# Taking turns between the two halves of an FFN chunk, product by product, in a streaming encoder layer

## The chip, the cores and the metric

The kernel runs on one core of a Trainium2 chip. The metric is device time in microseconds (us) for one launch: 2391.49 us before the change (median of three runs, 2389.07 to 2395.47).

## The reference

One Conformer-style layer for 1024 prompt frames and 32 sample frames, computed together as 1056 columns in fp32. The change touches only the two half-step FFNs, with D_MODEL 1024 and D_FF 2816:

```python
def _swiglu_half_step(x, g_pre, g_post, w_in, w_out):
    h = _rmsnorm(x, g_pre)
    gate, up = jnp.split(h @ w_in, 2, axis=-1)
    return x + 0.5 * _rmsnorm((jax.nn.silu(gate) * up) @ w_out, g_post)
...
x = _swiglu_half_step(x, g_ffn1_pre[l], g_ffn1_post[l], w_ffn1_in[l], w_ffn1_out[l])
# ... combined projection, conv branch, recurrent branch, merge ...
x = _swiglu_half_step(x, g_ffn2_pre[l], g_ffn2_post[l], w_ffn2_in[l], w_ffn2_out[l])
```

## The kernel before

All data is channels first: 128 channels on the partitions, columns (frames) along the free dimension. The 1056 columns are four quarters of 264. Every fp32 operand is split into a high and a low part (`split`: a copy by ScalarE, L91, then a subtraction by VectorE, L88), and every product is three matmuls, high by high, high by low, low by high (`mm3`, L202 to L204).

D_FF is cut into 22 chunks of 128 gate and 128 up channels. The first three chunks of FFN 1 (two of FFN 2) are ordinary products. The rest use a seven-product scheme on 2 x 2 blocks: the weight of a chunk (gate and up rows, two halves of the input channels) and the input (two halves of the input channels, an even and an odd quarter). `w_ops` makes seven weights w1 to w7 from the loaded rows w_g and w_u, by sums s and s3 on VectorE and a split each; w1, w2, w4 are blocks as loaded, w5, w6, w7, w3 need sums. `swiglu` does the seven products for one pair of quarters, called a half of the chunk here: 7 x 12 = 84 matmuls. Four PSUM tiles take part. p1 is product 1, then product 2 is added; p5 is product 5, copied to SBUF as s5; p6 starts as ScalarE's copy of p1 and gets product 6, then p7 starts as a copy of p6; VectorE adds s5 to p6; product 7 goes to p7, product 3 to p6, product 4 to p7. SiLU of p1 and p6 times the up values p7 and p7 + s5 (read after product 7) gives the hidden values `prod`, stored to DRAM (`hd`). `ffn` runs both halves of a chunk one after the other with the same weights, so a chunk is 168 matmuls. Then the output products read `hd` back (`hf`, split into hh and hl) with weights w_o.

What sets the order: the program's instructions are ordered by a scheduler that takes them by priority, which is the order of writing unless `tc.high_priority(offset=n)` moves an instruction up by n places, and by its own idea of when they are ready. On each engine they then run in exactly that order. Weight loads and weight splits have such offsets (`WAHEAD`, `WLATE`, `OAHEAD`); the copies and sums in PSUM have none. Pools limit what can be open: 6 PSUM banks for products, 3 raw weight buffers (a chunk takes two), 12 weight buffers (a chunk takes seven), 6 double tiles for weight sums and `prod`, 4 temporary tiles. All loads and stores are issued by SP's queue.

Of the kernel before, what the change touches and what calls it, by code (L numbers as in the profile page):

```python
# [10 lines left out]
AF = mybir.ActivationFunctionType  # L11
OP = mybir.AluOpType
# [8 lines left out]
N = T // NQ  # L21
# [11 lines left out]
UNIT = 1088  # L33
NU, NRING, NRAW, NTMP, NMID = 29, 12, 3, 4, 6

AHEAD, WAHEAD, WLATE, HAHEAD, OAHEAD = 350, 120, 100, 100, 150


SQ, TURN, CHAIN, MUW, LNW, STAG = 12, 6, 30, 16, 32, 32
# [13 lines left out]
def macaron_kernel(ctx: ExitStack, tc: tile.TileContext, a: dict, o: dict):  # L53
    nc = tc.nc
# [20 lines left out]
    def PAIR(dt, name):  # L75
        return up.tile([P, 2, 2 * N], dt, tag="u", name=name, padded_shape=[P, 2, UNIT // 2])

    def MID(name):
        return mp.tile([P, 2, N], F32, tag="m", name=name)

    def TMP(name):
        return tp.tile([P, N], F32, tag="t", name=name)

    def BANK(name):
        return ps.tile([P, 512], F32, tag="ps", name=name)

    def tt(out, x, y, op):
        return nc.vector.tensor_tensor(out, x, y, op=op)  # L88

    def copy(out, x):  # L90
        return nc.scalar.activation(out, x, AF.Copy)  # L91
# [27 lines left out]
    st = cp.tile([P, KC, H1 + H2 + 1], F32, name="st")  # L119
# [60 lines left out]
    def block(src, name, ahead=AHEAD, lead=0):  # L180
        with tc.high_priority(offset=ahead):
            with tc.high_priority(offset=lead):
                w = raw_block(src, name)
            h, l = (ring.tile([P, D], F32R, tag="r", name=f"w{x}_{name}") for x in "hl")
            split(h, l, w)
        return h, l
# [7 lines left out]
    def drain():  # L194
        while later:
            later.pop(0)[1]()
# [4 lines left out]
    def mm3(out, wh, wl, xh, xl, first, last):  # L201
        nc.tensor.matmul(out, wh, xh, start=first, stop=False, skip_group_check=True)  # L202
        nc.tensor.matmul(out, wh, xl, start=False, stop=False, skip_group_check=True)  # L203
        newest_mm[:] = [nc.tensor.matmul(out, wl, xh, start=False, stop=last, skip_group_check=True).ins]  # L204
        terms[0] += 1
        for e in [e for e in later if e[0] <= terms[0]]:
            later.remove(e)
            e[1]()
# [132 lines left out]
    def behind_parts(instructions):  # L341
        s = ExitStack()
        for ins in instructions:
            s.enter_context(tc.issue_after(ins))
        return s
# [50 lines left out]
            op("3", s)  # L396
        return r

    def swiglu(w, x, prod, name):

        def bank(k):
            return BANK(f"p{k}_{name}")[:, :N]

        def product(k, b, first):
            for j in range(HC):
                s = slice(j * P, (j + 1) * P)
                mm3(b, w[k][:, 0, s], w[k][:, 1, s], x[k][0][:, j, :], x[k][1][:, j, :], first and j == 0, j == HC - 1)  # L410

        s5, g0, g1, u1 = (TMP(f"{n}_{name}") for n in ("s5", "g0", "g1", "u1"))
        p1, p5 = bank("1"), bank("5")
        product("1", p1, True)
        p6 = bank("6")
        copy(p6, p1)
        product("5", p5, True)
        copy(s5, p5)
        product("6", p6, False)
        p7 = bank("7")  # L420
        copy(p7, p6)
        tt(p6, p6, s5, OP.add)
        product("2", p1, False)
        nc.scalar.activation(g0, p1, AF.Silu)
        product("7", p7, False)
        tt(u1, p7, s5, OP.add)
        product("3", p6, False)
        nc.scalar.activation(g1, p6, AF.Silu)  # L428
        product("4", p7, False)
        tt(prod[:, 1, :], g1, u1, OP.mult)  # L430
        return tt(prod[:, 0, :], g0, p7, OP.mult).ins


    def ffn(x, f, h, first, mid, w_in, w_out, early, between, finish, tail, n):
        hd = dp.tile([NF, P, T], F32, name=f"hd{n}")

        def hidden(i, w, c):
            prod = MID(f"prod{n}_{i}_{c}")
            last = swiglu(w, x[c], prod, f"{n}_{i}_{c}")
            nc.sync.dma_start(hd[i, :, 2 * N * c:2 * N * (c + 1)], prod)  # L440
            return last

        first(0, h)
        if n == 1:
            drain()
        q0 = list(newest_part) if n == 1 else []
        blks = []
        np = NP[n - 1]
        for i in range(np):
            with behind_parts(q0 if i else []):  # L450
                blks.append([block(w_in[2 * i + j], f"i{n}_{i}_{j}", AHEAD if n == 2 else 0, 2000 if n == 1 else 0) for j in range(2)])
        for q in range(NQ):
            if q + 1 < NQ:
                first(q + 1, h)
            if q not in h:
                drain()
            for i in range(np):
                pg = gemm(blks[i][0], h, q, f"pg{n}_{i}_{q}")
                pu = gemm(blks[i][1], h, q, f"pu{n}_{i}_{q}")
                t = TMP(f"si{n}_{i}_{q}")  # L460
                nc.scalar.activation(t, pg, AF.Silu)
                tt(t, t, pu, OP.mult)
                nc.sync.dma_start(hd[i, :, q * N:(q + 1) * N], t)
            if q >= 2:
                x_sums(x[q - 2], f[2 * q - 4], f[2 * q - 3], f"{n}_{q - 2}")
        for i in range(np, NF):
            with behind_parts(q0 if i == np else []):
                w = w_ops(w_in[2 * i], w_in[2 * i + 1], f"{n}_{i}", WAHEAD if i < np + 2 else WLATE)
            hidden(i, w, 0)
            end = hidden(i, w, 1)  # L470
            if i == 4:
                with tc.issue_after(end):
                    mid()

        sq = {}
        for c in range(2):
            hid = []
            for g in range(NF // 2):
                with tc.high_priority(offset=HAHEAD):
                    w = PAIR(F32, f"hf{n}_{c}_{g}")  # L480
                    nc.sync.dma_start(w, hd[2 * g:2 * g + 2, :, 2 * N * c:2 * N * (c + 1)].rearrange("k p n -> p k n"))
                    hi, lo = PAIR(F32R, f"hh{n}_{c}_{g}"), PAIR(F32R, f"hl{n}_{c}_{g}")
                    split(hi, lo, w)
                hid.append((hi, lo))
            y = {q: [QUAD(F32, f"y{n}_{q}_{h}") for h in range(2)] for q in (2 * c, 2 * c + 1)}
            for t in (t for q in y for t in y[q]):
                nc.gpsimd.memset(t[:, 0, 0:1], 0.0)
            if c == 1:
                for q in y0:
                    after(q * STAG, lambda q=q, y0=y0: early(q, y0[q], sq[q]))  # L490
            y0 = y

            def out(tiles, blks, which, c=c, hid=hid, y=y):

                b = {t: BANK(f"po{n}_{t[0]}_{t[1]}")[:, :N] for t in tiles}
                for k in range(NF):
                    hi, lo = hid[k // 2]
                    for m, q in tiles:
                        i = m * NF + k
                        if i // KC not in blks:  # L500
                            blks[i // KC] = block(w_out[i // KC], f"o{n}_{which}_{i // KC}", OAHEAD)
                        s = slice((q % 2) * N, (q % 2 + 1) * N)
                        mm(b[m, q], blks[i // KC], i % KC, hi[:, k % 2, s], lo[:, k % 2, s], k == 0, k == NF - 1)
                for m, q in tiles:
                    evacuate(y[q], m, b[m, q], half[:, n - 1, m:m + 1], sq, q, f"{n}_{q}_{m}")

            qs = (2 * c, 2 * c + 1)
            late = tail if c == 1 else 0
            both = {}
            out([(m, q) for m in range(OG) for q in qs], both, c)  # L510
            for m in range(OG, KC - late):
                for q in qs:
                    out([(m, q)], both, c)
                if c == 1 and m == HC - 1:
                    between()
            for q in qs:
                own = {}
                for m in range(KC - late, KC):
                    out([(m, q)], own, f"{c}_{q}")
                if c == 1 and q == 2:  # L520
                    finish(q, y[q], sq[q])
        return lambda: finish(3, y[3], sq[3])
# [146 lines left out]
    for i in range(KC):  # L669
        first, last = i == 0, i == KC - 1  # L670
# [21 lines left out]
        for k in range(H2):  # L692
            s = H2 - k
# [20 lines left out]
        for c0, cn in RCH:  # L714
            for j, dst in ((0, tau), (1, v)):
                b = BANK(f"pgt{i}_{c0}_{j}")[:, :cn]
# [29 lines left out]
        for q in range(NQ):  # L746
            p = gemm(br, hm, q, f"prg{i}_{q}")
            g = TMP(f"gl{i}_{q}")
            nc.scalar.activation(g, p, AF.Gelu_apprx_tanh)
            for lo, hi, to in pieces(q, H2):  # L750
                s = slice(to, to + hi - lo)
# [77 lines left out]
    for h in range(2):  # L829
        some = [co_row(h * HC + j) for j in range(HC)]  # L830
        for q in range(NQ):
            mg = QUAD(F32, f"mg{q}_{h}")
            s = slice(q * N, (q + 1) * N)
            for j, (b, g, r) in enumerate(some):
                p = gemm(b, hc, q, f"pco{h}_{j}_{q}")
# [107 lines left out]
```

## Time and profile before

| | before |
|---|---|
| runs (median, lowest, highest) | 2391.49, 2389.07, 2395.47 us |
| profiled execution | 2396.18 us, its span 2394.4 us |
| TensorE busy, granted clock | 2350.4 us (98%), mean 0.996 |
| VectorE, ScalarE busy | 1468.3 us (61%), 980.3 us (41%) |
| seven-product stage, FFN 1 and FFN 2 | 91.8 to 495.2 us, 1685.4 to 2108.7 us |

In the rows PE is TensorE, DVE VectorE, ACT ScalarE, SP the queue that issues loads and stores; times are us from the start of the span. A matmul's own duration (about 0.29 us) overlaps with the next ones, so the distance between starts is what counts. A name such as p<-xh,w is the written tile and the read ones, with numbers left out; all seven products have the name p. Idle time of an engine stands in square brackets with what ended it.

### The profile page before, as it was taken

How to read it: one execution, taken by the hardware profiler on the slowest of the kernel's cores; microseconds unless marked ns; L12 is line 12 of the kernel's file. 1: busy time of each engine (PE TensorE's matmuls, PEld its weight loads, DVE VectorE, ACT ScalarE, POOL GpSimd, SP SyncE). 2: the span in 40 equal slices, each digit the busy share in tenths (PEclk: the TensorE clock that was granted, in tenths of full speed). 3: DMA queues.
4: the chain of work that ended last, by engine and by line, in shares of the span. 5: the costliest groups of instructions: out<-in, count | busy, mean ns of one | idle time of the engine just before them, and what ended most of it. 6: DMA issues, size and time to landing. Idle time of an engine off the chain costs nothing.

```text
span 2394.4 us, 44896 instructions
## 1 busy us (share of the span) xinstructions
PE 2350.4 (98%) x19136; PEld 2332.3 (97%) x19136; DVE 1468.3 (61%) x2262; ACT 980.3 (41%) x1692; POOL 42.3 (2%) x63
## 2 busy tenths in 40 slices
PE   7999999999999999999999999999999999999996
PEld 7999999999999999999999999999999999999996
DVE  6754455442646887887778965558644455542646
ACT  4433333342444554345544343344433333442432
POOL 0000000000000000000000000001000000000000
PEclk9999999999999999999999999999999999999998
DMA  5122222263555222222222554444222222263453
GB/s 171 62 72 73 81 81 76 89 200 118 199 188 188 73 81 77 77 81 82 73 73 81 173 209 151 144 143 131 77 72 69 80 80 81 87 204 116 162 172 132
DMA packets 126088, 274.12 MB, mean 114 GB/s; under 512 B 16704, under 2 KB 58432, under 8 KB 125888
## 3 DMA queue, kind: packets, MB, share of 16 engines
q1 hardware_dynamic: 125888, 271.26, 34.5%
q8 instruction: 149, 2.44, 0.4%
q14 instruction: 51, 0.42, 0.1%
HBM read 212.55 MB, written 58.67 MB: 113 GB/s over the span
## 4 chain that ended last, share of the span: by engine, by line
PE 94%; DMA 2%; DVE 2%; issue 1%; ACT 1%; POOL 0%; SPq 0%; POOLq 0%; DVEq 0%; ACTq 0%
PE p L204 11%; PE p L202 11%; PE p L203 11%; PE po L203 7%; PE po L202 7%; PE po L204 7%; PE pm L202 3%; PE pm L204 3%; PE pm L203 3%; PE pcv L202 1%; PE pro L202 1%; PE pcg L202 1%; PE prx L202 1%; PE prg L202 1%; PE pcv L204 1%; PE pcg L204 1%
## 5 line engine op out<-in xcount | busy, mean ns | idle before, releaser
L202 PE MATMUL p<-xh,w 128*128 128x264 f32 x2184 | 627.8, 288 | 5.6 <-ACT p L91 5.3
L204 PE MATMUL p<-xh,w 128*128 128x264 f32 x2184 | 627.1, 289 | 0.1
L203 PE MATMUL p<-xl,w 128*128 128x264 f32 x2184 | 620.7, 285 | 0.0
L202 PEld LDWEIGHTS p<-xh,w 128*128 128x128 f32 x2184 | 413.1, 189 | 11.2 <-ACT p L91 6.9
L204 PEld LDWEIGHTS p<-xh,w 128*128 128x128 f32 x2184 | 411.8, 189 | 7.3 <-DVE w L88 1.5
L203 PEld LDWEIGHTS p<-xl,w 128*128 128x128 f32 x2184 | 414.1, 190 | 0.0
L203 PE MATMUL po<-hl,wh_o 128*128 128x264 f32 x1408 | 398.5, 285 | 0.5 <-DVE hl L88 0.5
L204 PE MATMUL po<-hh,wl_o 128*128 128x264 f32 x1408 | 397.1, 284 | 0.0
L202 PE MATMUL po<-hh,wh_o 128*128 128x264 f32 x1408 | 392.5, 286 | 0.8 <-ACT hh L91 0.8
L203 PEld LDWEIGHTS po<-hl,wh_o 128*128 128x128 f32 x1408 | 265.3, 189 | 1.2 <-DVE hl L88 1.2
L204 PEld LDWEIGHTS po<-hh,wl_o 128*128 128x128 f32 x1408 | 264.9, 188 | 0.0
L202 PEld LDWEIGHTS po<-hh,wh_o 128*128 128x128 f32 x1408 | 261.2, 189 | 1.5 <-ACT hh L91 1.5
L88 DVE TENSOR_TENSOR wl_o<-w_o,wh_o 128x1024 fp32r<-128x1024 f32 x109 | 133.1, 1224 | 118.8 <-ACT wh_o L91 115.5
L615 DVE SCALAR_TENSOR_TENSOR pq<-u,vec,pq 128x542 f32<-128x542 f32 (+14 forms) x232 | 171.1, 770 | 0.0
L91 ACT ACTIVATE wh_o<-w_o 128x1024 fp32r<-128x1024 f32 x109 | 115.5, 1063 | 119.8 <-PE po L203 113.5
L91 ACT ACTIVATE w<-s 128x512 fp32r<-128x512 f32 x156 | 94.2, 628 | 104.0 <-DVE s L88 101.5
L88 DVE TENSOR_TENSOR w<-s,w 128x512 fp32r<-128x512 f32 x156 | 104.1, 688 | 49.1 <-ACT w L91 49.1
L88 DVE TENSOR_TENSOR p<-p,s 128x264 f32<-128x264 f32 x78 | 34.1, 438 | 159.6 <-ACT p L91 159.6
L91 ACT ACTIVATE p<-p 128x264 f32<-128x264 f32 x156 | 58.4, 375 | 168.2 <-PE p L204 168.1
L428 ACT ACTIVATE g<-p 128x264 f32<-128x264 f32 x78 | 30.4, 390 | 147.5 <-PE p L204 147.5
L615 DVE SCALAR_TENSOR_TENSOR rs<-rs,wsum 128x542 f32<-128x542 f32 (+6 forms) x112 | 86.4, 771 | 0.0
L88 DVE TENSOR_TENSOR s<-s,s 128x264 f32<-128x264 f32 x56 | 24.0, 430 | 98.6 <-ACT s L313 98.5
(445 smaller groups left out, 5698.6 us busy)
## 6 DMA issues: line engine op xcount, KB each, us to landing
w_o<-in_w_ffn_out SPq DMA_DIRECT2D x109, 512.0 KB, 3.8
hf<-hd SPq DMA_DIRECT2D x44, 528.0 KB, 5.3
hd<-prod SPq DMA_DIRECT2D x78, 264.0 KB, 4.0
w_g<-in_w_ffn_in SPq DMA_DIRECT2D x39, 512.0 KB, 3.5
w_u<-in_w_ffn_in SPq DMA_DIRECT2D x39, 512.0 KB, 4.1
w_wo<-in_w_out SPq DMA_DIRECT2D x18, 512.0 KB, 3.5
sgd<-sg SPq DMA_DIRECT2D x32, 264.0 KB, 2.5
gs<-sgd SPq DMA_DIRECT2D x16, 528.0 KB, 6.8
```

The lines of the kernel that those rows point to most:

```text
L88: return nc.vector.tensor_tensor(out, x, y, op=op)
L91: return nc.scalar.activation(out, x, AF.Copy)
L202: nc.tensor.matmul(out, wh, xh, start=first, stop=False, skip_group_check=True)
L203: nc.tensor.matmul(out, wh, xl, start=False, stop=False, skip_group_check=True)
L204: newest_mm[:] = [nc.tensor.matmul(out, wl, xh, start=False, stop=last, skip_group_check=True).ins]
L428: nc.scalar.activation(g1, p6, AF.Silu)
L615: nc.vector.scalar_tensor_tensor(acc[c][:, d:], src[c][:, :HW - d], wt[c](d), acc[c][:, d:], op0=OP.mult, op1=OP.add)
```

## The change

`swiglu` now takes a list of columns (halves) and does each of the seven steps for every half before the next step. So product 1 of both halves, product 5 of both, then 6, 2, 7, 3, 4; a weight is used 24 matmuls in a row. The first seven-product chunk of each FFN keeps its halves apart. The copies and sums in PSUM and the SiLU of p1 get a priority offset of 200. SiLU of p1 is written into the result tile, as is p7 + s5, and product 3's SiLU is multiplied in place. The pools keep their sizes.

```diff
--- before.py
+++ after.py
@@ -33,7 +33,8 @@
 UNIT = 1088
 NU, NRING, NRAW, NTMP, NMID = 29, 12, 3, 4, 6
 
-AHEAD, WAHEAD, WLATE, HAHEAD, OAHEAD = 350, 120, 100, 100, 150
+
+AHEAD, WAHEAD, WLATE, HAHEAD, OAHEAD, EAHEAD = 350, 120, 100, 100, 150, 200
 
 
 SQ, TURN, CHAIN, MUW, LNW, STAG = 12, 6, 30, 16, 32, 32
@@ -396,48 +397,77 @@
             op("3", s)
         return r
 
-    def swiglu(w, x, prod, name):
-
-
-
-
-        def bank(k):
-            return BANK(f"p{k}_{name}")[:, :N]
-
-        def product(k, b, first):
+    def swiglu(w, cols, name):
+
+
+
+
+        st = [{} for _ in cols]
+
+        def soon():
+            return tc.high_priority(offset=EAHEAD)
+
+        def bank(c, k):
+            st[c][k] = BANK(f"p{k}_{name}_{c}")[:, :N]
+            return st[c][k]
+
+        def product(c, k, b, first):
+            x = cols[c][0]
             for j in range(HC):
                 s = slice(j * P, (j + 1) * P)
                 mm3(b, w[k][:, 0, s], w[k][:, 1, s], x[k][0][:, j, :], x[k][1][:, j, :], first and j == 0, j == HC - 1)
 
-        s5, g0, g1, u1 = (TMP(f"{n}_{name}") for n in ("s5", "g0", "g1", "u1"))
-        p1, p5 = bank("1"), bank("5")
-        product("1", p1, True)
-        p6 = bank("6")
-        copy(p6, p1)
-        product("5", p5, True)
-        copy(s5, p5)
-        product("6", p6, False)
-        p7 = bank("7")
-        copy(p7, p6)
-        tt(p6, p6, s5, OP.add)
-        product("2", p1, False)
-        nc.scalar.activation(g0, p1, AF.Silu)
-        product("7", p7, False)
-        tt(u1, p7, s5, OP.add)
-        product("3", p6, False)
-        nc.scalar.activation(g1, p6, AF.Silu)
-        product("4", p7, False)
-        tt(prod[:, 1, :], g1, u1, OP.mult)
-        return tt(prod[:, 0, :], g0, p7, OP.mult).ins
+        def step1(c, prod):
+            product(c, "1", bank(c, "1"), True)
+            with soon():
+                copy(bank(c, "6"), st[c]["1"])
+
+        def step5(c, prod):
+            product(c, "5", bank(c, "5"), True)
+            st[c]["s"] = TMP(f"s5_{name}_{c}")
+            with soon():
+                copy(st[c]["s"], st[c]["5"])
+
+        def step6(c, prod):
+            product(c, "6", st[c]["6"], False)
+            with soon():
+                copy(bank(c, "7"), st[c]["6"])
+                tt(st[c]["6"], st[c]["6"], st[c]["s"], OP.add)
+
+        def step2(c, prod):
+            product(c, "2", st[c]["1"], False)
+            with soon():
+                nc.scalar.activation(prod[:, 0, :], st[c]["1"], AF.Silu)
+
+        def step7(c, prod):
+            product(c, "7", st[c]["7"], False)
+            with soon():
+                tt(prod[:, 1, :], st[c]["7"], st[c]["s"], OP.add)
+
+        def step3(c, prod):
+            product(c, "3", st[c]["6"], False)
+            g = TMP(f"g1_{name}_{c}")
+            nc.scalar.activation(g, st[c]["6"], AF.Silu)
+            tt(prod[:, 1, :], prod[:, 1, :], g, OP.mult)
+
+        def step4(c, prod):
+            product(c, "4", st[c]["7"], False)
+            return tt(prod[:, 0, :], prod[:, 0, :], st[c]["7"], OP.mult).ins
+
+        for step in (step1, step5, step6, step2, step7, step3, step4):
+            for c, (_, prod) in enumerate(cols):
+                end = step(c, prod)
+        return end
 
 
     def ffn(x, f, h, first, mid, w_in, w_out, early, between, finish, tail, n):
         hd = dp.tile([NF, P, T], F32, name=f"hd{n}")
 
-        def hidden(i, w, c):
-            prod = MID(f"prod{n}_{i}_{c}")
-            last = swiglu(w, x[c], prod, f"{n}_{i}_{c}")
-            nc.sync.dma_start(hd[i, :, 2 * N * c:2 * N * (c + 1)], prod)
+        def hidden(i, w, cs):
+            cols = [(x[c], MID(f"prod{n}_{i}_{c}")) for c in cs]
+            last = swiglu(w, cols, f"{n}_{i}_{cs[0]}")
+            for c, (_, prod) in zip(cs, cols):
+                nc.sync.dma_start(hd[i, :, 2 * N * c:2 * N * (c + 1)], prod)
             return last
 
         first(0, h)
@@ -466,8 +496,8 @@
         for i in range(np, NF):
             with behind_parts(q0 if i == np else []):
                 w = w_ops(w_in[2 * i], w_in[2 * i + 1], f"{n}_{i}", WAHEAD if i < np + 2 else WLATE)
-            hidden(i, w, 0)
-            end = hidden(i, w, 1)
+            for cs in ((0,), (1,)) if i == np else ((0, 1),):
+                end = hidden(i, w, cs)
             if i == 4:
                 with tc.issue_after(end):
                     mid()
```

What this does to the order is shown at three places. In the names below the first number is the product or weight, then FFN, chunk and, for p, s5 and g, the half; w5_1_9 is the weight of product 5 of chunk 9 in FFN 1.

First, ScalarE around the weights of chunk 9. Before, from the last SiLU of chunk 8 on:

```order
L428 ACTIVATE g1_1_8_1_2390<-p6_1_8_1_2406 128x264 [waits DVE_49,PE_49]
L91 ACTIVATE w5_1_9_2505<-s_1_9_2503 128x512 [waits DVE_49]
L91 ACTIVATE p6_1_9_0_2540<-p1_1_9_0_2526 128x264 [waits PE_49]
L91 ACTIVATE w6_1_9_2509<-s_1_9_2503 128x512 [waits DVE_49]
L91 ACTIVATE w7_1_9_2515<-s3_1_9_2512 128x512
L91 ACTIVATE s5_1_9_0_2522<-p5_1_9_0_2527 128x264 [waits PE_49,Activation_49]
L91 ACTIVATE w3_1_9_2518<-s_1_9_2503 128x512 [waits DVE_49]
L91 ACTIVATE p7_1_9_0_2567<-p6_1_9_0_2540 128x264 [waits PE_49,Activation_49]
L91 ACTIVATE w1_1_10_2731<-w_g1_10_2727 128x512 [waits DMAHW7_49]
```

With the change, from the SiLU of product 2 of chunk 8 on:

```order
L440 ACTIVATE prod1_8_1_2265<-p1_1_8_0_1_2281 128x264 [waits DMAHW3_49,PE_49]
L92 ACTIVATE w5_1_9_2481<-s_1_9_2479 128x512 [waits DVE_49]
L92 ACTIVATE w6_1_9_2485<-s_1_9_2479 128x512 [waits DVE_49]
L92 ACTIVATE w7_1_9_2491<-s3_1_9_2488 128x512
L450 ACTIVATE g1_1_8_0_0_2420<-p6_1_8_0_0_2279 128x264 [waits PE_49]
L92 ACTIVATE w3_1_9_2494<-s_1_9_2479 128x512 [waits DVE_49]
L450 ACTIVATE g1_1_8_0_1_2435<-p6_1_8_0_1_2294 128x264 [waits PE_49]
L92 ACTIVATE w1_1_10_2703<-w_g1_10_2699 128x512 [waits DMAHW5_49]
L92 ACTIVATE w2_1_10_2706<-w_g1_10_2699 128x512
L92 ACTIVATE w4_1_10_2709<-w_u1_10_2701 128x512 [waits DMAHW0_49]
L92 ACTIVATE p6_1_9_0_0_2512<-p1_1_9_0_0_2499 128x264 [waits PE_49,Activation_49]
L92 ACTIVATE p6_1_9_0_1_2527<-p1_1_9_0_1_2514 128x264 [waits PE_49,Activation_49]
```

The high parts of w5, w6 and w7 of chunk 9 moved from behind the last SiLU of chunk 8 to ahead of both SiLUs on p6, and the copy p6<-p1 of chunk 9 now stands behind w4 of chunk 10, which waits for a load. VectorE's low parts and sums moved in the same way. On SP the load of w_u of a chunk and that of w_g of the next now follow each other directly; a store stood between them.

Second, TensorE where product 5 of chunk 5 begins. Before, from product 1's last matmul:

```order
L204 MATMUL p1_1_5_0_1578<-xh1_1_0_154,w1_1_5_1546 128x264
L202 MATMUL p5_1_5_0_1579<-xh5_1_0_817,w5_1_5_1557 128x264 [waits Activation_49]
L203 MATMUL p5_1_5_0_1579<-xl5_1_0_818,w5_1_5_1557 128x264
L204 MATMUL p5_1_5_0_1579<-xh5_1_0_817,w5_1_5_1557 128x264 [waits DVE_49]
L202 MATMUL p5_1_5_0_1579<-xh5_1_0_817,w5_1_5_1557 128x264
```

With the change, from the last matmul of product 1 of the second half:

```order
L205 MATMUL p1_1_5_0_1_1582<-xh1_1_2_497,w1_1_5_1538 128x264
L203 MATMUL p6_1_5_0_0_1580<-xh6_1_0_822,w6_1_5_1553 128x264 [waits Activation_49]
L203 MATMUL p5_1_5_0_0_1597<-xh5_1_0_817,w5_1_5_1549 128x264 [waits DVE_49]
L204 MATMUL p5_1_5_0_0_1597<-xl5_1_0_818,w5_1_5_1549 128x264
L205 MATMUL p5_1_5_0_0_1597<-xh5_1_0_817,w5_1_5_1549 128x264
```

One matmul of product 6 stands ahead of product 5, so the copy p6<-p1 is wanted 24 matmuls into the chunk, where it was wanted behind all of product 5 too; later matmuls no longer wait for the low part of w5.

Third, ScalarE at the start of chunk 21, the last one of FFN 1, where the output weights (wh_o) and hidden values (hh) come in. Before:

```order
L91 ACTIVATE w5_1_21_5349<-s_1_21_5347 128x512 [waits DVE_49]
L91 ACTIVATE hh1_0_0_5573<-hf1_0_0_5571 128x2x528 [waits PE_49]
L91 ACTIVATE w6_1_21_5353<-s_1_21_5347 128x512 [waits DVE_49]
L91 ACTIVATE w7_1_21_5359<-s3_1_21_5356 128x512
L91 ACTIVATE p6_1_21_0_5384<-p1_1_21_0_5370 128x264 [waits PE_49]
L91 ACTIVATE s5_1_21_0_5366<-p5_1_21_0_5371 128x264 [waits PE_49,Activation_49]
L91 ACTIVATE w3_1_21_5362<-s_1_21_5347 128x512 [waits DVE_49]
L91 ACTIVATE wh_o1_0_0_5651<-w_o1_0_0_5649 128x1024 [waits DMAHW7_49]
L91 ACTIVATE p7_1_21_0_5411<-p6_1_21_0_5384 128x264 [waits PE_49,Activation_49]
```

With the change:

```order
L450 ACTIVATE g1_1_20_0_0_5216<-p6_1_20_0_0_5075 128x264 [waits PE_49]
L92 ACTIVATE w3_1_21_5290<-s_1_21_5275 128x512 [waits DVE_49]
L450 ACTIVATE g1_1_20_0_1_5231<-p6_1_20_0_1_5090 128x264 [waits PE_49]
L92 ACTIVATE wh_o1_0_0_5575<-w_o1_0_0_5573 128x1024 [waits DMAHW5_49]
L92 ACTIVATE wh_o1_0_2_5587<-w_o1_0_2_5585 128x1024 [waits DMAHW0_49]
L92 ACTIVATE wh_o1_0_3_5617<-w_o1_0_3_5615 128x1024 [waits DMAHW1_49,PE_49]
L92 ACTIVATE hh1_0_0_5497<-hf1_0_0_5495 128x2x528 [waits PE_49]
L92 ACTIVATE p6_1_21_0_0_5308<-p1_1_21_0_0_5295 128x264 [waits PE_49,Activation_49]
L92 ACTIVATE p6_1_21_0_1_5323<-p1_1_21_0_1_5310 128x264 [waits PE_49,Activation_49]
```

The weights of chunk 21 are done earlier, and the copy p6<-p1 has three splits of output weights and one of hidden values directly in front of it, where there were weights of its own chunk and one split of hidden values.

## Rows read from the trace of the kernel before

**Rows 1.** The page: busy time by engine, and TensorE's granted clock by slices.

```profile
PE 2350.4 (98%) x19136; PEld 2332.3 (97%) x19136; DVE 1468.3 (61%) x2262; ACT 980.3 (41%) x1692; POOL 42.3 (2%) x63
PEclk9999999999999999999999999999999999999998
```

**Rows 2.** Stretches: length, busy time by engine (count), clock, DMA share, GB/s.

```profile
207.58:217.89 10.31, 10.31 (x86) 10.31 (x85) 2.15 (x5) 1.92 (x5) 0.00 (x0) 1.00 0.08 29
217.89:228.56 10.67, 10.67 (x87) 10.38 (x85) 8.02 (x15) 5.71 (x12) 0.00 (x0) 1.00 0.43 124
228.56:238.74 10.18, 10.18 (x87) 10.18 (x86) 2.14 (x5) 1.92 (x5) 0.00 (x0) 1.00 0.08 28
112.60:469.90 357.30, 357.30 (x2859) 352.13 (x2859) 176.86 (x371) 129.79 (x289) 1.67 (x1) 1.00 0.25 77
1705.70:2084.80 379.10, 379.10 (x3027) 373.64 (x3026) 183.16 (x343) 137.52 (x306) 0.00 (x0) 1.00 0.25 77
800.00:1400.00 600.00, 600.00 (x4950) 599.94 (x4949) 497.83 (x673) 280.77 (x437) 0.59 (x6) 1.00 0.29 97
```

**Rows 3.** Timeline at chunk 9's start (217.89), and the copy after its second half's product 1.

```profile
217.04 0.44 DVE L88 TENSOR_TENSOR prod<-g,u 128x264 f32<-128x264 f32 x1 [1.46 <-ACT g L428]
217.40 0.68 DVE L88 TENSOR_TENSOR s<-w_u 128x512 f32<-128x512 f32 x1
...
218.94 0.68 DVE L88 TENSOR_TENSOR w<-s,w 128x512 fp32r<-128x512 f32 x1
...
219.49 0.28 PE L203 MATMUL p<-xl,w 128*128 128x264 f32 x1
...
219.68 0.39 PE L204 MATMUL p<-xh,w 128*128 128x264 f32 x1
...
220.38 1.15 ACT L91 ACTIVATE w<-s 128x512 fp32r<-128x512 f32 x2 [0.44 <-DVE s L88]
...
221.06 0.39 PE L202 MATMUL p<-xh,w 128*128 128x264 f32 x1
...
230.22 0.38 ACT L91 ACTIVATE p<-p 128x264 f32<-128x264 f32 x1 [2.52 <-PE p L204]
```

**Rows 4.** Stretches: chunk 21, the last, of FFN 1 and of FFN 2.

```profile
469.89:495.20 25.31, 21.64 (x170) 20.66 (x169) 17.96 (x25) 15.19 (x24) 0.00 (x0) 1.00 0.71 221
2084.80:2108.70 23.90, 21.83 (x171) 20.86 (x170) 18.04 (x25) 15.39 (x24) 0.00 (x0) 1.00 0.73 237
```

**Rows 5.** Timeline in chunk 21 of FFN 1: SP, ScalarE and TensorE.

```profile
480.39 0.42 SPq L481 DMA_DIRECT2D hf<-hd  x1
...
488.12 1.08 ACT L91 ACTIVATE hh<-hf 128x1056 fp32r<-128x1056 f32 x1 [4.04 <-DMA hf<-hd]
...
490.75 0.39 PE L202 MATMUL p<-xh,w 128*128 128x264 f32 x1 [2.73 <-ACT p L91]
```

**Rows 6.** The page's groups: count | busy us, mean ns of one | idle before.

```profile
L91 ACT ACTIVATE w<-s 128x512 fp32r<-128x512 f32 x156 | 94.2, 628 | 104.0 <-DVE s L88 101.5
L88 DVE TENSOR_TENSOR w<-s,w 128x512 fp32r<-128x512 f32 x156 | 104.1, 688 | 49.1 <-ACT w L91 49.1
L88 DVE TENSOR_TENSOR p<-p,s 128x264 f32<-128x264 f32 x78 | 34.1, 438 | 159.6 <-ACT p L91 159.6
```

**Rows 7.** Loads: count, size, median us from issue to landing.

```profile
w_o<-in_w_ffn_out SPq DMA_DIRECT2D x109, 512.0 KB, 3.8
hf<-hd SPq DMA_DIRECT2D x44, 528.0 KB, 5.3
w_g<-in_w_ffn_in SPq DMA_DIRECT2D x39, 512.0 KB, 3.5
w_u<-in_w_ffn_in SPq DMA_DIRECT2D x39, 512.0 KB, 4.1
```

**Rows 8.** Timeline of SP in chunk 9.

```profile
218.75 0.33 SPq L172 DMA_DIRECT2D w_u<-in_w_ffn_in  x1
...
222.97 0.33 SPq L172 DMA_DIRECT2D w_g<-in_w_ffn_in  x1
```

## The prediction

> **What bounds the kernel now.** I read the page first: TensorE is busy for 98% of the span at a granted clock of 1.00 almost throughout, and no other engine passes 61% [rows 1]. Only time in which TensorE does not start a matmul can be won. A stretch in which nothing disturbs it gives the measure: 4950 matmuls in 600.00 us, 0.1212 us each [rows 2]. The change touches only the seven-product stage of the two FFNs. There the same count runs slower: the 17 chunks 4 to 20 of the first FFN hold 17 x 168 = 2856 matmuls and take 357.30 us, 21.02 us a chunk, and the 18 chunks 3 to 20 of the second take 379.10 us, 21.06 us a chunk [rows 2]. At 0.1212 us a chunk of 168 would be 20.36 us. The first half of a chunk (first pair of quarters) lasts 10.67 us and its second half 10.18 us with the same 84 matmuls [rows 2].
>
> The timeline of chunk 9's start says why [rows 3]. VectorE's low part of weight w5 ends at 219.62 (218.94 + 0.68), and the matmul that wants it starts at 219.68, 0.19 after the one at 219.49 and not 0.12. ScalarE's high part of w6 starts at 220.38 and takes half of 1.15; the matmul that wants it starts at 221.06, after the first of the two parts has come. These waits are real, short, and in the first half only, because the second half finds its weights ready. VectorE is late since the first sum of the weights (217.40) stands behind a product of chunk 8 that itself waited 1.46 us for ScalarE's silu. The longest waits lie in chunk 21, the last of each FFN, which takes 25.31 us in the first and 23.90 in the second [rows 4] where 20.36 would do: 8.5 us lost together. At 490.75 TensorE resumes after 2.73 us of waiting for a copy p7<-p6 that stood on ScalarE behind a split of hidden values, which waited 4.04 us for its load [rows 5].
>
> **The change part by part.** Number of operations: each half still has 84 matmuls, five ScalarE and four VectorE operations; SiLU of product 2 now writes straight into the result tile. This costs nothing.
>
> *The turns.* Each weight now serves both halves one after the other, so TensorE asks for a new weight every 24 matmuls (2.91 us) instead of every 12. What counts more is when the next chunk's weights are made. Take a chunk that starts at 0, products of 12 x 0.1212 = 1.455 us, and a lag of 0.20 us from a product's end to ScalarE's start (230.22 - 228.56 - 1.455) [rows 2, 3]. ScalarE takes 0.63 us for a high part, VectorE 0.69 us for a low part or a weight sum, sums in PSUM 0.44 us [rows 6], copies 0.38 (230.22 [rows 3]). In the new order the first weight sum of the next chunk stands on VectorE behind the two sums on p6, which end by 9.9; w5's high part follows ScalarE's second SiLU of product 2 (11.85 + 0.39) and ends at 12.9; w6 and w7 follow the two VectorE sums after product 7 and are whole by 16.5; w3's last sum ends at 17.2 and its low part at about 18.8. All of it is ready before 20.36, the next chunk's start, and w5 is wanted only at 23.3. So the 0.49 us (10.67 - 10.18) per chunk go: 35 x 0.49 = 17.2 us. That is the term I take. Its upper bound is the whole distance to the undisturbed rate, 17 x (21.02 - 20.36) + 18 x (21.06 - 20.36) = 23.8 us; but the 6.6 us between the two are a slightly slower matmul rate without a wait (a second half of 10.31 us beside one of 10.18 [rows 2]), which nothing in the change addresses.
>
> *What is late next.* One matmul of product 6 now stands before product 5, 24 matmuls into the chunk. It wants the copy p6<-p1, and this copy stands on ScalarE behind w4's high part of the chunk after, which waits for the load of w_u. That load can start when the raw buffer of w_g is read for the last time, at 17.2; SP issues it then (0.1). With the median landing of 4.1 us [rows 7] w4 splits from 21.4 to 22.0, the copy runs from 22.05 (its product ended at 21.8) to 22.4, and TensorE wants it at 20.36 + 2.91 = 23.3. Margin 0.8 us: no wait. The landing is the uncertain part, since the change also puts w_g's load directly behind w_u's where they were 4.2 us apart (218.75 and 222.97 [rows 8]). Its bounds: 3.5 us (w_g) and 7.7 us (a hidden load issued at 480.39 among weight loads, and used at 488.12) [rows 5, 7]. At 5.3 us (the median of hidden loads) the wait would be 0.3 us a chunk. I take 4.1, whose row is the same load.
> On queue order the Trainium skill ("DMA: Bandwidth & Descriptors", Queues, rings and completion order) says that each DMA engine consumes descriptors in the order of its ring, so a load behind w_u's should not slow it. By this rule the landing stays at 4.1 us and the sum stands; if the two loads shared the engines evenly instead, it is the second rival below.
>
> *The last chunk.* Here the higher priority acts on the order, but not as one would wish: in front of p6<-p1 stand three splits of output weights and one of hidden values (1.08 us for a split of this kind [rows 5]). w_o_0_2 and w_o_0_3 are issued together at -3.2 (last read of w_g of chunk 21) and land, 3.8 us later for the first [rows 7] and 2.2 more for the second (512 KB at the 237 GB/s of that chunk in the second FFN [rows 4]), at 0.6 and 2.8. Splits to 3.85, hidden split to 4.9, copy to 5.3 where TensorE wants it at 2.9: 2.4 us late, in either FFN. Later copies and sums have 1 us or more in hand after that delay. So 8.5 - 2 x 2.4 = 3.7 us gained. Bounds: no wait at all (8.5 gained), and the second load landing 7.7 us after its issue, a wait of 4.1 us twice (0.3 gained).
>
> *PSUM.* Both halves open four tiles each, eight in six banks. p5 of the next chunk takes the bank of p7, free once VectorE's final product is done, by 23.3 for the second one at the latest; TensorE wants it at 20.36 + 3 x 1.455 = 24.7. Covered by 1.4 us, so nothing.
>
> Sum: 17.2 + 3.7 = 20.9 us. The profiled execution took 2396.18 us (span 2394.4 and 1.8 around it), 4.7 above the median of the three runs, 2391.49. 2396.18 - 20.9 = 2375.3; carried over to the median, 2370.6, rounded 2371 us. Bounds together: 23.8 + 8.5 = 32.3 gained (2359), and, with half of the 0.49 us left in each chunk and the long load in the last, 8.6 + 0.3 = 8.9 gained (2383).
>
> **Rivals.** *The banks or the single matmul take back what the weights give.* If w_u lands in 5.5 us, the copy is 0.5 us late in each of 35 chunks and the gain of 17.2 is gone; with the last chunks at their worse bound the time is 2391. For it: ScalarE's copy of p6 now has two queues ahead of it. Against: 0.8 us of margin and a DMA share of 0.25 in this stage [rows 2]. The Trainium skill ("Perfetto Trace Analysis", Optimization Strategy) states that a gap which repeats can mean too little PSUM or SBUF for the next tile; by this rule more open tiles in six banks would lengthen the gap. The trace speaks against it here, since every repeated gap ends with a weight part of VectorE or ScalarE.
>
> *Slower: the two loads share the engines.* If w_g's data runs beside w_u's, w_u's transfer doubles: an estimated 2.2 of its 4.1 us are data (512 KB at 237 GB/s again), so it lands in 6.3. The copy then ends at 24.6, 1.3 us late, in every chunk: 35 x (1.3 - 0.49) - 3.7 = 24.7 us lost, 2416. It turns slower from a landing of 5.6 us on. For it: the 7.7 us row. Against: that load stood behind two others, which order alone explains.
>
> *Only the last chunk changes*: if the 0.49 us were no weight wait but belonged to the first half as such, 3.7 us would stay, 2388. Rows 3 speak against it: the ends and starts match to 0.1 us.
>
> **How the numbers follow.** Forecast (2359 to 2383): 0.78. Gain gone or only the last chunk (2384 to 2398): 0.13. Slower by shared loads or a worse last chunk: 0.09. A change of less than 0.3%, 7 us, is no change for this kernel, whose three runs spread over 6 us. Faster 0.80 (the forecast and a part of the second case), same 0.11, slower 0.09. The range, 2359 to 2388, is the forecast's own with the last-chunk case at its high end, and leaves out the rest.
>
> **What would show it.** In the profile after, both FFN stages should hold chunks of 20.4 to 20.7 us without first-half gaps; matmuls on w5, w6 and w7 should not wait for VectorE or ScalarE; one wait of 1 to 4 us should stand in each last chunk, 24 matmuls in, for the copy p6<-p1. I am wrong if a gap repeats 24 matmuls into each chunk behind w_u's load, or 36 into it behind VectorE's final product.

## The result, and the profile after

| | before | changed |
|---|---|---|
| runs (median, lowest, highest) | 2390.39, 2389.07, 2395.47 us (4 runs) | 2360.61, 2359.78, 2361.00 us (4 runs) |
| profiled execution, span | 2396.18, 2394.4 us | 2361.00, 2359.2 us |

The ratio is 0.9871, 95% interval 0.9854 to 0.9888: 29.8 us less, where 2371 was forecast from 2391.49 (20 less). The time lies inside the range of 2359 to 2388, near its low end. The two profiled executions differ by 35.2 us, since the one of before lies 5.8 above its median.

Stretches of the changed kernel: first the chunks 4 to 20 and the chunk 21 of FFN 1, then 3 to 20 and 21 of FFN 2, and two single chunks, 4 and 9 of FFN 1. The columns are those of [rows 2]: of the figures with a count, the first is TensorE's matmuls, the second its weight loads. A count takes in the two or three matmuls that a window's ends cut.

```profile
112.34:458.50 346.16, 346.16 (x2859) 346.16 (x2857) 175.60 (x375) 133.13 (x293) 1.67 (x1) 1.00 0.24 80
458.50:479.00 20.50, 20.50 (x171) 20.41 (x169) 12.46 (x17) 11.58 (x18) 0.00 (x0) 1.00 0.75 259
1687.43:2053.94 366.51, 366.51 (x3026) 366.51 (x3025) 180.40 (x347) 140.92 (x310) 0.00 (x0) 1.00 0.24 80
2053.94:2074.44 20.50, 20.50 (x170) 20.41 (x169) 10.74 (x15) 10.46 (x18) 0.00 (x0) 1.00 0.74 247
112.34:132.87 20.53, 20.53 (x170) 20.53 (x169) 12.95 (x25) 9.79 (x22) 0.00 (x0) 1.00 0.28 90
214.34:234.69 20.35, 20.35 (x171) 20.35 (x170) 9.84 (x20) 7.69 (x17) 0.00 (x0) 1.00 0.23 79
```

Set beside [rows 2, 4], this says where the time came from. The busy time of the weight loads is now the whole stretch: no matmul waits between chunk 4 and chunk 20 of FFN 1, or chunk 3 and chunk 20 of FFN 2. The clock is 1.00 on both sides.

| stretch | before | changed | less |
|---|---|---|---|
| chunks 4 to 20 of FFN 1 | 357.30 | 346.16 | 11.1 |
| chunks 3 to 20 of FFN 2 | 379.10 | 366.51 | 12.6 |
| chunk 21 of FFN 1 | 25.31 | 20.50 | 4.8 |
| chunk 21 of FFN 2 | 23.90 | 20.50 | 3.4 |

Together 31.9 us of the 35.2. Of the other 3.3, some 2 lie in a stage that the change does not touch. The same stretch of 130 us, first of before and then of the changed kernel:

```profile
1452.00:1582.00 130.00, 129.86 (x1058) 129.65 (x1058) 59.76 (x101) 39.71 (x61) 0.00 (x0) 1.00 0.37 129
```

```profile
1434.00:1564.00 130.00, 130.00 (x1075) 129.97 (x1074) 61.41 (x104) 41.26 (x63) 0.00 (x0) 1.00 0.38 134
```

In the first, 1058 matmuls fit into 130 us (0.1229 us each), in the second 1075 (0.1209). TensorE is busy for all but 0.14 us of the first, so this is hardly a wait but a slower distance between matmuls; I come back to it.

VectorE in chunk 9 (start 214.34) shows how early the weights of chunk 10 are now. The columns are start, duration, engine, line and operation, written tile and read tiles.

```profile
223.72 0.44 DVE L89 TENSOR_TENSOR p<-p,s 128x264 f32<-128x264 f32 x1 [1.01 <-ACT p L92]
224.07 0.68 DVE L89 TENSOR_TENSOR s<-w_u 128x512 f32<-128x512 f32 x1
224.66 0.69 DVE L89 TENSOR_TENSOR s<-w_g,w_u 128x512 f32<-128x512 f32 x1
...
227.11 0.69 DVE L89 TENSOR_TENSOR w<-s,w 128x512 fp32r<-128x512 f32 x1 [1.76 <-ACT w L92]
...
229.44 1.29 DVE L89 TENSOR_TENSOR w<-s,w 128x512 fp32r<-128x512 f32 x2
230.65 0.69 DVE L89 TENSOR_TENSOR s<-w_g,s 128x512 f32<-128x512 f32 x1
...
232.03 0.69 DVE L89 TENSOR_TENSOR w<-s,w 128x512 fp32r<-128x512 f32 x1 [0.35 <-ACT w L92]
```

The first weight sum stands directly behind the second sum on p6, at 9.7 us into the chunk; it was at 217.40, half a microsecond before the chunk that needs it [rows 3]. The low part of w5 ends at 227.80, those of w6 and w7 at 230.73, that of w3 at 232.72. Chunk 10 begins at 234.69.

The page's loads, for the step on w_u [rows 7]:

```profile
w_g<-in_w_ffn_in SPq DMA_DIRECT2D x39, 512.0 KB, 3.5
w_u<-in_w_ffn_in SPq DMA_DIRECT2D x39, 512.0 KB, 3.4
```

And SP in chunk 9:

```profile
225.41 0.33 SPq L173 DMA_DIRECT2D w_u<-in_w_ffn_in  x1
231.37 0.33 SPq L173 DMA_DIRECT2D w_g<-in_w_ffn_in  x1
```

The two loads follow each other in the queue, but 5.96 us apart, and w_u lands faster than before, not slower (3.4 against 4.1).

### The profile page after: what moved, and what is told of

Same layout as the page of the kernel before. It is cut to its first block, busy times and chain, and to the rows that moved or that the text cites. A ratio compares the mean times of both kernels' runs of the same rounds, so it can differ in the third digit from the quotient of the medians.

```text
span 2359.2 us, 44813 instructions
## 1 busy us (share of the span) xinstructions
PE 2321.7 (98%) x19136; PEld 2316.2 (98%) x19136; DVE 1457.2 (62%) x2262; ACT 981.9 (42%) x1692; POOL 43.1 (2%) x63
## 4 chain that ended last, share of the span: by engine, by line
PE 94%; DVE 2%; DMA 1%; issue 1%; ACT 1%; POOL 0%; SPq 0%; POOLq 0%; DVEq 0%
PE p L203 11%; PE p L205 11%; PE p L204 11%; PE po L204 7%; PE po L203 7%; PE po L205 7%; PE pm L203 3%; PE pm L205 3%; PE pm L204 3%; PE pco L203 1%; PE pcv L203 1%; PE pro L203 1%; PE pcg L203 1%; PE prx L203 1%; PE prg L203 1%; PE pcv L205 1%
## 5 line engine op out<-in xcount | busy, mean ns | idle before, releaser
L205 PE MATMUL p<-xh,w 128*128 128x264 f32 x2184 | 618.6, 284 | 0.0
L203 PE MATMUL p<-xh,w 128*128 128x264 f32 x2184 | 615.6, 285 | 0.0
L89 DVE TENSOR_TENSOR hl<-hf,hh 128x1056 fp32r<-128x1056 f32 x44 | 55.2, 1255 | 45.7 <-ACT hh L92 45.6
```

## The experiments

The change has three parts: the turns, the priority offset, and the temporaries that were given up (SiLU of p1 and p7 + s5 go into the result tile). My theory (A): what counts is when the next chunk's weights are whole against when they are wanted; the turns make them wanted later, the missing temporaries make them earlier, and either is enough. Rivals: the priority does it (e1), the turns alone (B, e2), the earlier sums alone (C, e3). The first four share their runs of before, with a median of 2392.61 us (2388.18 to 2394.62); e7 has its own, with 2392.93 us (2390.74 to 2395.81).

**e1, no priority.**

```diff
-AHEAD, WAHEAD, WLATE, HAHEAD, OAHEAD, EAHEAD = 350, 120, 100, 100, 150, 200
+AHEAD, WAHEAD, WLATE, HAHEAD, OAHEAD, EAHEAD = 350, 120, 100, 100, 150, 0
```

> The changed kernel with the priority offset of the copies and sums set to 0. Theory: the offset moves almost nothing (the order of ScalarE and SyncE stays as it is, VectorE's differs at one place in the first seven-product chunk of each FFN), so the time is that of the changed kernel, 2361 us, within 2 us. Rival: the higher priority of the copies is what removes the waits; then the time goes towards 2390 us.

Measured: 2362.82 us (2359.06 to 2363.27), ratio 0.9870 (0.9853 to 0.9886). The stage, FFN 1 and FFN 2:

```profile
112.84:459.03 346.19, 346.19 (x2858) 346.19 (x2857) 175.64 (x375) 133.20 (x293) 1.67 (x1) 1.00 0.24 80
1689.23:2055.74 366.51, 366.51 (x3026) 366.51 (x3025) 180.46 (x347) 140.99 (x310) 0.00 (x0) 1.00 0.24 80
```

To 0.03 us the stretches of the changed kernel, and chunk 21 takes the same 20.50 us in FFN 1 (20.49 in FFN 2). The priority is worth nothing here; the rival falls. The stage at 1436 to 1565 us had the slower distance in this execution as in before:

```profile
1436.00:1565.00 129.00, 129.00 (x1053) 129.00 (x1052) 59.85 (x101) 39.81 (x61) 0.00 (x0) 1.00 0.37 129
```

That is 0.1225 us a matmul without a wait, which is some 1.7 us over the 0.1209 of the changed kernel and about the 1.6 us by which this execution was longer.

**e2, halves apart, fewer temporaries.**

```diff
-            for cs in ((0,), (1,)) if i == np else ((0, 1),):
+            for cs in ((0,), (1,)):
```
(and the offset 0 as in e1)

> The changed swiglu, with its fewer temporaries, but every chunk keeps its halves apart; no priority offset. Theory A (the weights of the next chunk are made earlier, and either part of the change alone is enough for that): the first half of a chunk loses nothing, as SiLU of product 3 and the product behind it come after the first weight sums on VectorE; chunks of 20.36 us. In chunk 21 the copy p7<-p6 of the second half still stands behind a hidden split and an output split, so the stall of 2.9 and 1.3 us stays: 2361 + 4.2 = 2365 us. Theory B (the turns alone do it, since a weight is then wanted 24 matmuls later): first halves lose 0.47 us in 35 chunks as before, 2361 + 16 + 4 to 8 = 2381 to 2390 us.

Measured: 2364.96 us (2362.43 to 2366.37), ratio 0.9882 (0.9867 to 0.9896). Chunk 5 and chunk 21 of FFN 1, then the chunks 3 to 20 and 21 of FFN 2:

```profile
132.80:155.03 22.23, 20.98 (x170) 20.56 (x169) 14.57 (x67) 7.40 (x18) 1.67 (x1) 1.00 0.23 73
...
460.23:481.68 21.45, 20.90 (x171) 20.48 (x169) 15.60 (x21) 13.72 (x22) 0.00 (x0) 1.00 0.71 238
1689.81:2056.05 366.24, 366.24 (x3026) 366.24 (x3025) 184.79 (x343) 133.62 (x307) 0.00 (x0) 1.00 0.25 79
2056.05:2077.88 21.83, 20.89 (x171) 20.47 (x169) 15.70 (x21) 13.72 (x22) 0.00 (x0) 1.00 0.71 233
```

The 18 chunks of FFN 2 have 20.35 us each without the turns: theory B falls, and with it the idea that this gain needs a weight to serve 24 matmuls in a row. The total came out as expected, but by luck, since its parts did not. Chunk 21 loses 1.1 and 1.5 us, not 2.9 and 1.3; and chunk 5 of FFN 1 loses 1.9 us that I had not seen. There VectorE has 67 instructions, among them the constants of the middle stage, and TensorE waits 0.7 us for the sum on p6 and 0.6 us for p7 + s5, which stand among them. ScalarE in chunk 21:

```profile
474.56 1.09 ACT L92 ACTIVATE hh<-hf 128x1056 fp32r<-128x1056 f32 x1 [1.79 <-DMA hf<-hd]
475.55 0.37 ACT L92 ACTIVATE s<-p 128x264 f32<-128x264 f32 x1
475.82 1.05 ACT L92 ACTIVATE wh_o<-w_o 128x1024 fp32r<-128x1024 f32 x1
476.77 0.38 ACT L92 ACTIVATE p<-p 128x264 f32<-128x264 f32 x1
```

The same queue as in [rows 5] (hidden split, s5, output split, then p7<-p6), where ScalarE waited 1.79 us for the hidden load instead of 4.04. So the last chunks gain some 6 us without the turns. By the profiles the turns are worth some 4 us more, in these three chunks; the runs don't settle it, since the range of e2 overlaps those of e1 and e3.

**e3, turns with the old temporaries.**

```diff
-NU, NRING, NRAW, NTMP, NMID = 29, 12, 3, 4, 6
+NU, NRING, NRAW, NTMP, NMID = 29, 12, 3, 5, 6
...
-                nc.scalar.activation(prod[:, 0, :], st[c]["1"], AF.Silu)
+                st[c]["g"] = TMP(f"g0_{name}_{c}")
+                nc.scalar.activation(st[c]["g"], st[c]["1"], AF.Silu)
...
-                tt(prod[:, 1, :], st[c]["7"], st[c]["s"], OP.add)
+                st[c]["u"] = TMP(f"u1_{name}_{c}")
+                tt(st[c]["u"], st[c]["7"], st[c]["s"], OP.add)
...
```

> Turns and priorities as in the changed kernel, but SiLU of p1 and p7 + s5 go to temporaries of their own again (5 temporary tiles instead of 4). The first weight sum of the next chunk stands again behind a product with SiLU of p6 on VectorE. Theory A: w5 is whole at about 20.4 us after the chunk's start, where it is wanted at 23.3, so there are no waits and the time is 2361 us, within 2 us. Theory C (the earlier order of the sums alone does it): waits of 0.3 to 0.5 us in 35 chunks return, 2371 to 2380 us.

Measured: 2361.54 us (2358.80 to 2362.97), ratio 0.9867 (0.9852 to 0.9882). VectorE at the end of chunk 9 (213.52 to 233.80):

```profile
231.53 0.43 DVE L89 TENSOR_TENSOR prod<-g,u 128x264 f32<-128x264 f32 x1 [1.01 <-ACT g L452]
231.88 0.68 DVE L89 TENSOR_TENSOR s<-w_u 128x512 f32<-128x512 f32 x1
...
233.42 0.69 DVE L89 TENSOR_TENSOR w<-s,w 128x512 fp32r<-128x512 f32 x1
```

and the stage:

```profile
111.51:457.32 345.81, 345.69 (x2859) 345.48 (x2857) 179.94 (x373) 129.42 (x290) 1.66 (x1) 1.00 0.26 79
457.32:477.89 20.57, 20.57 (x171) 20.57 (x169) 15.53 (x21) 12.98 (x21) 0.00 (x0) 1.00 0.83 268
1685.40:2051.50 366.10, 365.98 (x3027) 365.76 (x3025) 186.16 (x345) 137.11 (x307) 0.00 (x0) 1.00 0.26 79
```

The first sum stands behind the product with SiLU again, as in before, and the low part of w5 ends at 234.11, 20.6 us into the chunk (20.4 expected). It is wanted at 233.80 + 2.91 = 236.7, and nothing waits; the 0.33 us without a weight load in each stretch lie in its first chunk, the first with turns. Theory C falls: later weights do no harm as long as they are wanted later still. With before, e2 and the changed kernel all four combinations are measured, and only the one without either part has the repeated waits. One thing is not separated: e3 has five temporary tiles where before has four (its priority offset is worth nothing by e1), and before was not run with five.

**e4, turns in the first chunk as well.**

```diff
-            for cs in ((0,), (1,)) if i == np else ((0, 1),):
+            for cs in ((0, 1),):
```

> The changed kernel with the first seven-product chunk of each FFN also taking turns. If the slower matmul distance (122.8 instead of 121.1 ns) in the first chunk after it comes from the step from halves apart to turns, it goes or moves to the chunk before, and 0.5 us at most are won: 2360 us. If a wait appears in the first chunk, 2362 us.

Measured: 2361.08 us (2359.88 to 2361.86), ratio 0.9866 (0.9851 to 0.9881). The chunks 4 to 20 of FFN 1 take 345.89 us:

```profile
111.86:457.75 345.89, 345.89 (x2858) 345.89 (x2857) 172.08 (x369) 131.02 (x288) 1.67 (x1) 1.00 0.23 79
```

0.27 us less than in the changed kernel, whose slower chunk 4 (20.53 us) is gone here, and has not moved to chunk 3. In FFN 2 the first chunk with turns, chunk 2, waits instead: it takes 20.86 us, against 20.60 in the changed kernel. Too little to show in the runs.

**e5 and e6, the two kernels without an edit, profiled again.**

> The kernel before, profiled a second time, for the slower matmul distance (122.7 instead of 121.1 ns) without waits. If it follows from the short waits of the first halves, it stands again in most of the chunks 4 to 20 of both FFNs and costs 6 to 8 us there. If it is chance of one execution, the chunks in which it stands are others, and the sum differs by some us. Whole run 2389 to 2396 us.

> The changed kernel, profiled a second time. If the slower distance follows from short waits, the seven-product stage has it at no more than 3 of the 39 chunks again; if it is chance, it may stand anywhere, for several us. 2359 to 2363 us.

Measured, one run each: 2394.20 us for the kernel before, 2360.63 for the changed one. From e5 the stages, and the two chunks 21:

```profile
111.76:469.00 357.24, 357.24 (x2858) 352.06 (x2857) 176.75 (x371) 129.79 (x289) 1.67 (x1) 1.00 0.25 77
1702.91:2081.07 378.16, 378.16 (x3027) 372.73 (x3026) 183.07 (x343) 137.54 (x306) 0.00 (x0) 1.00 0.25 77
469.00:493.10 24.10, 21.65 (x171) 20.68 (x170) 17.99 (x25) 15.33 (x24) 0.00 (x0) 1.00 0.75 234
2081.07:2105.00 23.93, 21.77 (x170) 20.81 (x169) 17.31 (x24) 14.65 (x24) 0.00 (x0) 1.00 0.75 236
```

The stages are within 1 us of [rows 2]; chunk 21 of FFN 1 is 1.2 us shorter than in [rows 4]. Taking each chunk's mean distance without the matmuls that waited, 30 of the 35 chunks lie above 122 ns in the first profile of before and 26 in the second, and not the same ones: chunk 17 is slow in the first and fast in the second. In the changed kernel both profiles have the same two slow chunks in part, 4 in FFN 1 and 3 in FFN 2 (20.54 us), each with an end that reaches into the next. So in the FFN stages the slow distance goes with the kernel that waits, and chance has a hand in which chunks have it. It is not bound to that kernel: outside these stages e1 has it too. What starts it in the changed kernel, where no wait stands ahead of it, stays open; it stands at the same two places in both profiles and in e1, and in neither profile without the step from halves apart to turns (e4, e7).

**e7, turns in every chunk with the old temporaries:** the edits of e3 and e4 together.

> Turns in every chunk together with the old temporaries (5 temporary tiles): the two variants with the smallest losses together. The chunks that had 120.74 instead of 121.11 ns a matmul give 17 x 0.06 = 1 us, the first chunk 0.3 to 0.5: 2359.5 us, against 2361 if these parts don't add. Less than the runs spread, so hardly to be told from the changed kernel.

Measured: 2360.14 us (2359.67 to 2362.87), ratio 0.9865 (0.9849 to 0.9881). As expected not to be told from the changed kernel; no version tried beats it by what the runs can show.

## Why the prediction was right, and where its sizes were wrong

- *The waits in the first halves go.* Right, and by the mechanism named. The first weight sum comes behind the two sums on p6 (predicted to end by 9.9 us into the chunk, measured 9.8), the high part of w5 ends at 12.9 by the forecast and just before 227.11, 12.8 into the chunk, in the trace; w6 and w7 are whole at 16.5 against 16.4, w3 at 18.8 against 18.4. What I did not see is that this step stands on two legs, each enough alone for the repeated waits (e2, e3). I took the early weights as a matter of the turns.
- *The term that failed most:* "the 6.6 us between the two are a slightly slower matmul rate without a wait ..., which nothing in the change addresses". The chunks 4 to 20 and 3 to 20 lost 23.7 us together, nearly all of the 23.8 that I gave as the upper bound, where 17.2 were taken. The slower distance went with the waits. The order of matmuls alone does not make it: the kernel before has chunks at both distances in one order, and e2, which keeps its order but for some 210 of 19,036 matmuls, has no slow chunk left in FFN 2. That the waits bring it is the likelier reading: no run put short waits into a kernel without them, but in an unchanged stage the distance changed at a late matmul, in either direction (last section).
- *The last chunk.* The place was right, the size and the reason were not: a wait for the copy p6<-p1, 24 matmuls in, was to take 2.4 us. I put this order on ScalarE down to the higher priority; e1 has the same order without it. TensorE in chunk 21 of FFN 1, and then ScalarE ahead of it:

```profile
461.28 0.28 PE L205 MATMUL p<-xh,w 128*128 128x264 f32 x1
461.45 0.52 PE L203 MATMUL p<-xh,w 128*128 128x264 f32 x2
```

```profile
456.08 2.00 ACT L92 ACTIVATE wh_o<-w_o 128x1024 fp32r<-128x1024 f32 x2
458.70 1.06 ACT L92 ACTIVATE wh_o<-w_o 128x1024 fp32r<-128x1024 f32 x1 [0.62 <-PE p L205]
460.03 1.09 ACT L92 ACTIVATE hh<-hf 128x1056 fp32r<-128x1056 f32 x1 [0.27 <-PE p L204]
461.03 0.37 ACT L92 ACTIVATE p<-p 128x264 f32<-128x264 f32 x1
```

  The order is the one shown ahead of the prediction, three output splits and a hidden one in front of the copy. The copy ends at 461.40, 2.9 us into the chunk, just when it is wanted: the matmul starts 0.05 us late, and the next one 0.11 (0.15 us in each FFN). I had two loads of w_o issued together, 3.2 us before the chunk, and the last split at 3.85 us into it. SP issued the first at 449.23, 9.3 us before the chunk:

```profile
449.23 6.29 SPq L173 DMA_DIRECT2D w_o<-in_w_ffn_out  x2
...
455.19 0.33 SPq L173 DMA_DIRECT2D w_o<-in_w_ffn_out  x1
```

  the second at 455.19, 3.3 us before, as I had it, and the last split ended at 459.76, 1.3 us into the chunk. So 8.2 us came from the last chunks, not 3.7; again near the upper bound (8.5). Against the second profile of before (24.10 and 23.93 us) it is 7.0.
- *The w_u load.* Right in its result (no wait), wrong in the working, so that the result was luck here. I had the load wait for the last read of w_g's buffer, at 17.2. That read (s<-w_g,s) does end 17.0 us into the chunk, at 231.34, but what SP issues behind it is a w_g (231.37). The load of w_u goes out at 225.41, 11.1 us into the chunk, right behind the last read of w_u itself (s<-w_g,w_u, to 225.35), and w4 is split at 233.31, 19 us into the chunk. The first of the two w_o loads above is early in the same way: 449.23 is 11.1 us into chunk 20, and 455.19 is 17.0. From 225.41 even the 6.3 us of the rival with shared engines would have ended at 231.7, so that rival had no ground. Queue order as the Trainium skill tells it ("DMA: Bandwidth & Descriptors", Queues, rings and completion order) was not put to the test, since the loads were 6 us apart.
- *Eight tiles in six banks* cost nothing, as forecast: no matmul of the chunks 4 to 20 of FFN 1 or 3 to 20 of FFN 2 waits.
- Sum: 31.9 us in the stage by the profile, 20.9 forecast, 32.3 as the upper bound. Both open terms had come out of "least that is sure", and both lay near their other end. The bound was reckoned from the same execution of before; with the second profiles (e5, e6) the stage gains 29.7 us, and the runs 29.8. The range held because its low end was that bound; the sum itself missed by a third.

## What to carry to other kernels

When short waits repeat in every pass of a loop, count with them everything that is slow in the same stretch, and compare it with an undisturbed stretch: here the bound from the rate (23.8 us) was the better forecast than the sum of the waits (17.2). Before a change with several parts is credited to one of them, run each alone; here two parts were each enough for the repeated waits, only the turns removed the rest, and the third did nothing. Where a stall hangs on loads, read when each buffer comes free before two of them are put down to the same moment.

## What the runs showed of the hardware that was not expected

- The mean distance between matmuls of the same shape has steady values at a clock of 1.00, mostly about 121.1 or 122.8 ns, and a stretch keeps one of them for up to 130 us. e3 even alternates between 121.1 and 120.7 from chunk to chunk. The chunks 9 and 8 of FFN 1 in e3:

```profile
213.52:233.80 20.28, 20.28 (x170) 20.28 (x169) 10.27 (x20) 7.59 (x17) 0.00 (x0) 1.00 0.25 79
193.17:213.52 20.35, 20.35 (x171) 20.35 (x169) 10.29 (x20) 7.59 (x17) 0.00 (x0) 1.00 0.26 81
```

- The distance can change at a late matmul. In the middle stage, which no edit touches, two of the nine profiles change it, e5 to the slow and e6 to the fast value, first the two stretches of e5, then those of e6:

```profile
1449.00:1503.00 54.00, 54.00 (x449) 54.00 (x447) 25.51 (x45) 14.27 (x18) 0.00 (x0) 1.00 0.35 124
1504.00:1579.00 75.00, 75.00 (x613) 75.00 (x613) 34.70 (x58) 26.61 (x45) 0.00 (x0) 1.00 0.39 133
...
1433.00:1488.00 55.00, 55.00 (x451) 55.00 (x450) 25.84 (x44) 14.65 (x18) 0.00 (x0) 1.00 0.35 125
1489.00:1544.00 55.00, 55.00 (x457) 55.00 (x456) 28.21 (x48) 18.45 (x28) 0.00 (x0) 1.00 0.42 146
```

  Between the stretches a matmul starts 0.10 us late (e5, at 1503.34) or two start 0.06 and 0.10 late (e6, at 1488.51 and 1488.74). In three other profiles a late matmul at this place leaves the distance as it was, and in the four without one it does not change.

- A wait of under 0.1 us can cost more than its length: in the first halves of before, the matmul behind the waiting one is late as well, by about 0.10 us. In chunk 9 of before, the matmul at 219.68 [rows 3] was 0.07 us late, and the one after it started 0.22 us later:

```profile
219.90 0.29 PE L202 MATMUL p<-xh,w 128*128 128x264 f32 x1
```

  It is not so everywhere: in the middle stage of the changed kernel the matmul at 1489.06 starts 0.09 us late, and the next one on time, at 1489.18.
